# Block products of a seven-product matrix scheme chained in PSUM: banks copied by ScalarE and added to by further products, in place of sums on VectorE

## The chip, the cores and the metric

The kernel runs on one core of a Trainium2 chip. The metric is the device time of one execution in microseconds. A few words that are used throughout: PE is TensorE (the matrix unit), DVE is VectorE, ACT is ScalarE, POOL is GpSimd, SP is the engine that issues most transfers. PSUM is the memory that PE's products land in, in banks of 128 x 512 floats; SBUF is the working memory that everything else reads and writes.

## What is computed

The reference is one inference step of a two-layer decoder trunk on 512 prompt tokens and 64 sample tokens (576 in all), with a model width of 1024 and a branch width of 2048. Layer 0 is a gated short convolution, layer 1 an mLSTM block with a matrix memory. What matters here are the large projections:

```
# layer 0
b_gate, c_gate, xa, z = split(rmsnorm(x) @ w_in, 4)      # 1024 -> 4 x 2048
u = c_gate * xa;  y = b_gate * causal_conv(u) * silu(z);  x = x + y @ w_out
# layer 1
xm, z = split(rmsnorm(x) @ b_w_in, 2)
xc = silu(causal_conv(xm) + bias)
q = xc @ w_q;  k = xc @ w_k;  v = xm @ w_v               # 2048 -> 2048 each
... gates, chunkwise mLSTM with the states C, n, m, head norm, skip, silu(z), w_out ...
```

All arithmetic is in float32. PE multiplies rounded operands here, so each float32 operand is written as a rounded high part and a low part (`hi`, `lo`), and a product is three matmuls: hi by hi, hi by lo, lo by hi.

## The kernel before

Activations are kept transposed: a tile has 128 channels on the partitions and the 576 tokens along the free dimension. Everything is written for one core with a framework that gives each engine an instruction order of its own; the order is set by a list scheduler that works on the program's text and on its own estimates, so that an instruction of one engine can stand earlier or later than the source has it.

**Plain projections.** `products` (L222) runs 8 blocks of 128 input channels, three matmuls each, and each in two pieces (256 and 320 tokens), so 48 matmuls for one group of 1024 input channels and 128 output channels. The weights come by transfer as 128 x 1024 tiles (`wr`); ScalarE rounds them (`wh`, L202) and VectorE subtracts to get the low part (`wl`, L203). Four buffers hold `wh`, four `wl`, so a cast waits until PE has used the tile of four casts earlier.

**Pairs by seven block products.** For 38 pairs of output tiles the kernel uses a scheme that replaces eight half-size products by seven. Tokens are cut into two halves of 288 (`HT`), the input channels of a group of 1024 into even and odd blocks, and the two output tiles are the two rows of a 2 x 2 block matrix. `block_weights` loads the two weight tiles (a11, a12 in the first, a21, a22 in the second) and makes the sums s1 = a21 + a22 and s2 = s1 + a11 on VectorE (L286, L287); `mixed` and `forms` make the matching sums t1 to t4 of the activations. `block_pair` then runs the seven products of 12 matmuls each (4 blocks, three matmuls, 288 tokens; the inner function `product`, L304), every one with its own cast (`parts_of`, L250) and low part (L251). The results o11, o12 (first output tile) and o21, o22 (second) are, with P1 = a11 b11:

```
o11 = P1 + a12 b21
o12 = P1 - s2 t2 + s1 t1 + (s2 + a12) b22
o22 = s2 t2 + (a21 + a11) t3 - P1 - s1 t1
o21 = s2 t2 + (a21 + a11) t3 - P1 + a22 t4
```

(the signs are those of this kernel's sums). Before the change P1 is copied to SBUF (`p`, L311, ScalarE), products that only ever add are chained in one PSUM bank (`a12 b21` after P1 in `b0`, `t3` after `t2` in `b1`, `b22` after `t1` in `b2`), and everything else is added by VectorE from PSUM (L316 to L358).

There are three uses. In layer 0, 14 pairs (f = 1 to 14, `xs is None`): a pair gives c_gate and xa for 128 channels, then come two plain projections (`product(2)`, `product(3)`: z and b_gate) and the convolution, whose steps are taken from a list (`work`) by `run`, which `block_pair` calls between products. In layer 1, 8 pairs give v and 16 give k and q (the first of the 16 has `add`); there the other 1024 input channels are added by `plain` (L368), 48 matmuls per output tile into the same banks, and each finished tile is transposed on PE (`by_token`, L680 and L682) after GpSimd has spread the sample tokens (`spread`, L671).

PSUM is handed out by `accumulators`: a new pool per stage, with four banks of tag `blk` for the pairs. At the end of f = 0 in layer 0 and before the v stage a new pool with the same four banks is opened.

## Time and profile before

| | |
|---|---|
| three timed runs | 1714.5, 1715.65, 1722.03 us (median 1715.65) |
| the profiled execution's own time | 1715.56 us |
| its span, first to last instruction | 1713.5 us |
| PE busy in it | 1669.4 us (97%), 12315 matmuls |
| VectorE, ScalarE, GpSimd busy | 1105.3, 685.3, 107.7 us (65%, 40%, 6%) |
| mean granted PE clock | 0.987 of full speed |
| layer 0 pairs, from the profile's rows | about 51 to 375 us |
| v stage, then k and q stage | 612 to 820 us, 820 to 1284 us |

How to read it. Busy PE time says only that a matmul was in flight: matmuls overlap, one lasts about 294 ns while a new one starts every 133 ns or so (2260 of them in the 300 us from 100 to 400 us), and so the number of matmuls in a stretch of time tells more than the busy share. The trace writes a group of instructions as line, engine, operation, output from input, count, busy time, mean duration, idle time before it and what ended that idle time. A few matmul records can be missing from a trace.

### The profile page before, as it was taken

What the parts mean: (1) busy time and instruction counts of PE and PEld (TensorE: products, weight loads), DVE (VectorE), ACT (ScalarE), POOL (GpSimd) and SP (SyncE); (2) the same over time, 40 slices, a digit from 0 to 9 for tenths busy, and PEclk for the clock granted to TensorE, in tenths of its full rate; (3) what the DMA queues carried; (4) which work ended last, traced back from release to release, by engine and by line L of the source; (5) the groups of instructions that cost most, each with busy time, mean ns of one, the idle gap of its engine ahead of it and who ended that gap; (6) DMA issues with size and microseconds to landing.
All of it is one profiled execution on the core that took longest, in us unless ns stands there. A gap on an engine that the chain in (4) does not pass through costs nothing.

```text
span 1713.5 us, 30944 instructions
## 1 busy us (share of the span) xinstructions
PE 1669.4 (97%) x12315; PEld 1591.1 (93%) x12315; DVE 1105.3 (65%) x2078; ACT 685.3 (40%) x1252; POOL 107.7 (6%) x241
## 2 busy tenths in 40 slices
PE   9999999999999999999999999999999998898998
PEld 8999999999999999999999889899899787898898
DVE  6977877774436896555846345355468556778755
ACT  5433343342323553433534233233246455554421
POOL 0000000000000001000110010000021000000000
PEclk9999999999999999999999999999999899999999
DMA  5223322223432434434423552642745588797973
GB/s 193 74 83 99 103 86 85 90 73 137 141 115 87 141 122 151 138 111 154 152 88 120 188 178 87 219 154 62 271 161 195 201 280 286 247 361 249 362 276 105
DMA packets 107487, 275.23 MB, mean 161 GB/s; under 512 B 11056, under 2 KB 33456, under 8 KB 107344
## 3 DMA queue, kind: packets, MB, share of 16 engines
q1 hardware_dynamic: 91984, 255.95, 45.0%
q10 hardware_dynamic: 15360, 17.32, 2.9%
q8 instruction: 97, 1.59, 0.4%
q14 instruction: 46, 0.38, 0.1%
HBM read 211.13 MB, written 62.09 MB: 159 GB/s over the span
## 4 chain that ended last, share of the span: by engine, by line
PE 88%; DMA 5%; DVE 4%; ACT 2%; issue 1%; SPq 0%; POOL 0%; DVEq 0%; ACTq 0%; POOLq 0%
PE acc L222 34%; PE p L304 24%; PE p L368 16%; DMA c<-cs 2%; PE qa L759 2%; PE r L1122 2%; DMA cs_out<-c 1%; DMA wr<-wts 1%; PE g L661 1%; PE num L1175 1%; PE ta L680 1%; PE cp L1175 1%; PE num L1176 1%; PE s L778 1%; PE blk L368 1%
## 5 line engine op out<-in xcount | busy, mean ns | idle before, releaser
L222 PE MATMUL acc<-hi,wh 128*128 128x256 f32 (+1 forms) x1520 | 331.7, 299 | 11.1 <-ACT z L875 6.8
L222 PE MATMUL acc<-hi,wl 128*128 128x256 f32 (+1 forms) x1520 | 330.8, 299 | 0.0
L222 PE MATMUL acc<-lo,wh 128*128 128x256 f32 (+1 forms) x1520 | 330.2, 299 | 0.0
L202 ACT CAST wh<-wr 128x512 fp32r<-128x512 f32 x286 | 176.5, 621 | 328.6 <-PE acc L222 174.5
L304 PE MATMUL p<-hi,wh 128*128 128x288 f32 x968 | 286.7, 299 | 3.7 <-ACT wh L250 2.1
L304 PE MATMUL p<-lo,wh 128*128 128x288 f32 x968 | 284.5, 295 | 0.0
L304 PE MATMUL p<-hi,wl 128*128 128x288 f32 x968 | 279.2, 295 | 1.2 <-DVE wl L251 1.2
L222 PEld LDWEIGHTS acc<-hi,wh 128*128 128x128 f32 x1520 | 257.8, 191 | 16.0 <-ACT z L875 7.0
L203 DVE TENSOR_TENSOR wl<-wr,wh 128x512 fp32r<-128x512 f32 x286 | 195.8, 689 | 118.4 <-ACT wh L202 115.8
L222 PEld LDWEIGHTS acc<-hi,wl 128*128 128x128 f32 x1520 | 257.8, 191 | 2.2 <-issue 1.2
L222 PEld LDWEIGHTS acc<-lo,wh 128*128 128x128 f32 x1520 | 257.7, 191 | 0.7 <-issue 0.5
L250 ACT CAST wh<-wr 128x512 fp32r<-128x512 f32 x152 | 94.5, 622 | 258.4 <-PE p L368 116.7
L304 PEld LDWEIGHTS p<-hi,wh 128*128 128x128 f32 x968 | 181.9, 188 | 7.8 <-ACT wh L250 3.7
L304 PEld LDWEIGHTS p<-lo,wh 128*128 128x128 f32 x968 | 182.4, 188 | 0.0
L304 PEld LDWEIGHTS p<-hi,wl 128*128 128x128 f32 x968 | 179.9, 188 | 1.4 <-DVE wl L251 1.4
L368 PE MATMUL p<-hi,wh 128*128 128x288 f32 x736 | 169.9, 299 | 0.0
L368 PE MATMUL p<-lo,wh 128*128 128x288 f32 x736 | 166.9, 294 | 0.0
L368 PE MATMUL p<-hi,wl 128*128 128x288 f32 x736 | 166.4, 296 | 0.2 <-DVE wl L203 0.2
L251 DVE TENSOR_TENSOR wl<-ws,wh 128x512 fp32r<-128x512 f32 x114 | 78.7, 691 | 119.6 <-ACT wh L250 119.4
L250 ACT CAST wh<-ws 128x512 fp32r<-128x512 f32 x114 | 70.8, 621 | 187.8 <-PE p L368 108.3
L251 DVE TENSOR_TENSOR wl<-wr,wh 128x512 fp32r<-128x512 f32 x152 | 104.9, 691 | 52.3 <-ACT wh L250 50.5
L368 PEld LDWEIGHTS p<-hi,wh 128*128 128x128 f32 x736 | 120.8, 188 | 14.7 <-issue 11.2
(371 smaller groups left out, 2557.2 us busy)
## 6 DMA issues: line engine op xcount, KB each, us to landing
wr<-wts SPq DMA_DIRECT2D x222, 512.0 KB, 3.6
c<-cs SPq DMA_DIRECT2D x112, 512.0 KB, 5.8
cs_out<-c SPq DMA_DIRECT2D x64, 512.0 KB, 6.7
x<-xT SPq DMA_DIRECT2D x16, 288.0 KB, 4.1
xcs<-xc ACTq DMA_DIRECT2D x16, 288.0 KB, 2.2
x<-xcs SPq DMA_DIRECT2D x16, 288.0 KB, 4.1
x<-x1s SPq DMA_DIRECT2D x16, 288.0 KB, 4.5
ld<-xcs SPq DMA_DIRECT2D x16, 288.0 KB, 7.5
```

The costliest lines, as they stand in the source:

```text
L202: last_act[0] = nc.scalar.copy(hi, raw[:, 4 * i:4 * i + 4, :]).ins
L203: nc.vector.tensor_tensor(lo, raw[:, 4 * i:4 * i + 4, :], hi.bitcast(F32), ALU.subtract)
L222: nc.tensor.matmul(acc[:, o:o + j - i], a[:, k % 4, :], x[:, i:j], start=(first and k == 0 and p == 0), stop=(last and k == 7 and p == 2))
L250: last_act[0] = nc.scalar.copy(hi, src).ins
L251: nc.vector.tensor_tensor(lo, src, hi.bitcast(F32), ALU.subtract)
L304: nc.tensor.matmul(bank_, a[:, j, :], x, start=(start and j == 0 and i == 0), stop=(j == 3 and i == 2), skip_group_check=True)
L368: nc.tensor.matmul(b, a[:, k % 4, :], x[:, t:t + HT], start=bool(new) and k == 0 and i == 0, stop=(k == 7 and i == 2), skip_group_check=True)
L661: nc.tensor.matmul(g[32 * j:32 * j + 32, 0:b - a], w[:, 32 * j:32 * j + 32], tiles[j][:, a:b], start=True, stop=True)
L680: nc.tensor.transpose(pa[:, 128 * it:128 * it + 128], t[:, 128 * it:128 * it + 128], ident)
L759: nc.tensor.matmul(st["q"][32 * g:32 * g + 32, :], st["qp"][dt // 2][:, dt % 2, 128 * u + 32 * g:128 * u + 32 * g + 32], ct[g // 2][:, g % ...
L1122: nc.tensor.matmul(r, kst[2 * i + j][:, 128 * dt:128 * dt + 128], vst[:, 0:512], start=True, stop=True)
L1175: nc.tensor.matmul(acc[:, 256:512], w, b[:, 0:256], **ends)
```

## The change

In `block_pair` the order of the products is new and three banks hold running sums. P1 goes to bank `bx`. ScalarE writes its negative into a second bank (`by`, L310 of the new kernel), and the products with t2, t3 and t4 are added to `by` by PE one after the other; between them ScalarE copies what `by` holds at that time (`u` at L318, and `p` at L325 or a fourth bank `bv` at L328). s1 t1 goes to a third bank (`bw`), is copied to a new SBUF tile `m5` (L315), and gets the product with b22 added. Of the sums from PSUM two a pair remain on VectorE (six in the one pair with `add`). In the v, k and q stages both halves of `plain` now add to banks that are already in use (`bx` with `bw`, `by` with `bv`). `mark` writes one product into each of the four banks of a new pool, twice in the program, so that later products without a start flag add to what ScalarE wrote there.

```
-            b1 = block("p6")
-            product(b1, parts_of(s2), "t2", True)
-            b0 = block("p1")
-            product(b0, parts_of(a11), "b11", True)
-            nc.scalar.copy(p, b0)
+            bx = block("p1")
+            product(bx, parts_of(a11), "b11", True)
+            by = block("p6")
+            nc.scalar.activation(by, bx, AF.Copy, scale=-1.0)
             run(pops)
-            b2 = block("p5")
-            product(b2, parts_of(s1), "t1", True)
-            (sums of o12 from p and b1)
+            bw = block("p5")
+            product(bw, parts_of(s1), "t1", True)
+            m5 = X(HT, name="m5")
+            nc.scalar.copy(m5, bw)
+            run(pops)
+            product(by, parts_of(s2), "t2", False)
+            nc.scalar.copy(u, by)
+            tt(s2, s2, a12, ALU.add)
+            product(bx, parts_of(a12), "b21", False)
+            tt(a21, a21, a11, ALU.add)
+            run(pops)
+            product(by, parts_of(a21), "t3", False)
+            if xs is None or add:
+                nc.scalar.copy(p, by)
+            else:
+                bv = block("p7")
+                nc.scalar.copy(bv, by)
+            product(bw, parts_of(s2), "b22", False)
             run(pops)
-            product(b0, parts_of(a12), "b21", False)
...
-            b3 = block("p4")
-            product(b3, parts_of(a22), "t4", True)
-            tt(u, b1, p, ALU.subtract)
...
+            product(by, parts_of(a22), "t4", False)
...
+            if xs is None:
+                tt(o22, p, m5, ALU.subtract)
+                nc.scalar.copy(o11, bx)
+                tt(o12, bw, u, ALU.subtract)
+                nc.scalar.copy(o21, by)
+                return
+            plain(bx, bw, c1 + 1, xs, None)
+            nc.scalar.copy(o11, bx)
+            tt(o12, bw, u, ALU.subtract)
+            plain(by, bv, c2 + 1, xs, None)
+            nc.scalar.copy(o21, by)
+            tt(o22, bv, m5, ALU.subtract)
+
+        def mark(w, x):
+
+            for b in [block("mark") for _ in range(4)]:
+                nc.tensor.matmul(b, w, x, start=True, stop=True)
...
                 accumulators("acc0a", bufs=2)
+                mark(h1[0][0][:, 0:P], h1[0][0][:, 0:HT])
...
         accumulators("acc1", bufs=4)
+        mark(xm[0][0][:, 0:P], xm[0][0][:, 0:HT])
```

How the orders of the engines move is shown at three places. In the rows, a name's digits are buffer numbers, `p` is a PSUM bank of a pair, and the brackets name the engines that the instruction waits for. First PE at the end of f = 0 in layer 0, where the first pair begins. Before, `p_700` is the bank of s2 t2, `p_717` of P1 and `p_737` of s1 t1:

```order
L222 MATMUL acc_584<-hi_265,wl_592 128x320
L304 MATMUL p_700<-hi_405,wh_701 128x288 [waits PE_49,Activation_49]
L304 MATMUL p_700<-lo_406,wh_701 128x288
L304 MATMUL p_717<-hi_137,wh_718 128x288 [waits Activation_49]
L304 MATMUL p_717<-lo_138,wh_718 128x288
L304 MATMUL p_737<-hi_405,wh_738 128x288 [waits Activation_49]
```

After, on the same place, with `p_708` the bank of P1:

```order
L222 MATMUL acc_584<-hi_265,wl_592 128x320
L361 MATMUL mark_672<-hi_137 128x288 [waits Activation_49]
L361 MATMUL mark_673<-hi_137 128x288
L361 MATMUL mark_674<-hi_137 128x288
L361 MATMUL mark_675<-hi_137 128x288
L304 MATMUL p_708<-hi_137,wh_709 128x288 [waits PE_49]
L304 MATMUL p_708<-lo_138,wh_709 128x288
L304 MATMUL p_708<-hi_137,wl_710 128x288 [waits DVE_49]
```

The first pair used to begin with two matmuls each of three products, s2's first; now it begins with four marks and with the whole of P1, whose weights and activations need none of the sums.

Second, ScalarE in one pair in the middle of layer 0. Before, `pu` (L311) is the copy of P1, `cv` the convolution, `z` the gate, `wh` the weight casts:

```order
L250 CAST wh_2716<-wr_2496 128x512 [waits DMAHW3_49,PE_49,Activation_49]
L159 CAST hi_2622<-cv_2351 128x576 [waits DVE_49]
L250 CAST wh_2735<-wr_2496 128x512 [waits PE_49,Activation_49]
L311 COPY pu_2637<-p_2655 128x288 [waits PE_49]
L250 CAST wh_2755<-ws_2500 128x512 [waits PE_49,Activation_49]
L436 ACTIVATE cv_2630<-u_2629,cols 128x576 [waits DVE_49,Pool_49]
L202 CAST wh_2783<-wr_2631 128x512 [waits DMAHW5_49,PE_49,Activation_49]
L350 COPY cx_2635<-p_2655 128x288 [waits PE_49]
```

After, the same stretch of a pair (`p_2384` is the bank `by`, `p_2367` is `bx`, `p_2388` is `bw`; L310 writes `by`, L318 and L325 read it):

```order
L250 CAST wh_2446<-wr_2228 128x512 [waits DMAHW7_49,PE_49,Activation_49]
L310 ACTIVATE p_2384<-p_2367 128x288 [waits PE_49]
L159 CAST hi_2354<-cv_2083 128x576 [waits DVE_49]
L250 CAST wh_2463<-ws_2232 128x512 [waits PE_49,Activation_49]
L315 COPY m_2405<-p_2388 128x288 [waits PE_49]
L439 ACTIVATE cv_2359<-u_2358,cols 128x576 [waits DVE_49]
L250 CAST wh_2481<-wr_2228 128x512 [waits PE_49,Activation_49]
L318 COPY pu_2366<-p_2384 128x288 [waits PE_49]
L202 CAST wh_2512<-wr_2360 128x512 [waits DMAHW0_49,PE_49,Activation_49]
L202 CAST wh_2516<-wr_2360 128x512 [waits DVE_49,PE_49]
L202 CAST wh_2572<-wr_2362 128x512 [waits DMAHW1_49,PE_49]
L325 COPY pu_2366<-p_2384 128x288 [waits PE_49]
```

ScalarE's copies now stand between the casts and the two activations that wait for VectorE, and PE waits for three of them (L310, L318, L325) before it adds to `by`. PE's own order goes with that: the products run as P1, s1, s2, a12, s2 + a12, a21, that is with 12 matmuls between P1 and the first product on `by`, 24 between the first and the second, and the last (t4) stands some 27 matmuls behind the second, in the middle of the plain projection that follows.

Third, PE where one v pair ends and the next begins. Before, these transposes of the finished pair (`ta` from `v`, `tb` from the spread samples `dup`) come after three products of the next pair; `v_8244` and `v_8245` are its two output tiles:

```order
L304 MATMUL p_8596<-hi_6341,wl_8598 128x288
L680 MATMUL ta_8714<-cst,v_8244 128x128 [waits Activation_49]
L680 MATMUL ta_8714<-cst,v_8244 128x128 x3
L682 MATMUL tb_8715<-cst,dup_8552 128x128 [waits PE_49,Pool_49]
L682 MATMUL tb_8715<-cst,dup_8552 128x128 [waits Pool_49]
L680 MATMUL ta_8740<-cst,v_8245 128x128 [waits PE_49]
```

After, they come behind the first product (`p_8577` is the next pair's `bx`):

```order
L304 MATMUL p_8577<-hl_6357,wl_8579 128x288
L684 MATMUL ta_8730<-cst,v_8260 128x128 [waits Activation_49]
L684 MATMUL ta_8730<-cst,v_8260 128x128 x3
L686 MATMUL tb_8731<-cst,dup_8568 128x128 [waits Pool_49]
L684 MATMUL ta_8756<-cst,v_8261 128x128 [waits DVE_49,Activation_49]
L684 MATMUL ta_8756<-cst,v_8261 128x128
L684 MATMUL ta_8756<-cst,v_8261 128x128 [waits DVE_49]
```

The transposes moved 24 matmuls nearer to the end of the pair whose results they read, and the second tile, which is now the one finished last, is read only a few matmuls behind the first. Behind the last pair of the k and q stage the program's text is the same as before, and the orders differ there by groups of a few matmuls that stand earlier or later.

More of the change, by code (lines that the diff above doesn't have):

```diff
@@ L305, in product @@
                                          skip_group_check=True)
-            b1 = block("p6")
-            product(b1, parts_of(s2), "t2", True)
-            b0 = block("p1")
-            product(b0, parts_of(a11), "b11", True)
-            nc.scalar.copy(p, b0)
-            run(pops)
-            b2 = block("p5")
-            product(b2, parts_of(s1), "t1", True)
-            if add:
-                tt(o12, o12, b1, ALU.subtract)
-                tt(o12, o12, p, ALU.add)
-            else:
-                tt(o12, p, b1, ALU.subtract)
+            bx = block("p1")
+            product(bx, parts_of(a11), "b11", True)
+            by = block("p6")
+            nc.scalar.activation(by, bx, AF.Copy, scale=-1.0)
+            run(pops)
+            bw = block("p5")
[12 more added lines that the diff above has]
+                nc.scalar.copy(p, by)
+            else:
+                bv = block("p7")
+                nc.scalar.copy(bv, by)
+            product(bw, parts_of(s2), "b22", False)
             run(pops)
-            product(b0, parts_of(a12), "b21", False)
-            if add:
-                tt(o22, o22, b2, ALU.subtract)
-                tt(o22, o22, p, ALU.subtract)
-            else:
-                tt(o22, p, b2, ALU.add)
-            tt(a21, a21, a11, ALU.add)
-            tt(s2, s2, a12, ALU.add)
-            run(pops)
-            product(b1, parts_of(a21), "t3", False)
-            run(pops)
-            b3 = block("p4")
-            product(b3, parts_of(a22), "t4", True)
-            tt(u, b1, p, ALU.subtract)
-            if add:
-                tt(o22, o22, b1, ALU.add)
-            else:
-                tt(o22, b1, o22, ALU.subtract)
-            run(pops)
-            product(b2, parts_of(s2), "b22", False)
+            product(by, parts_of(a22), "t4", False)
+            run(pops)
             if mid:
@@ L345, in block_pair @@
             if add:
-                tt(o11, o11, b0, ALU.add)
-                tt(o21, o21, b3, ALU.add)
-                tt(o21, o21, u, ALU.add)
-            elif xs is None:
-                nc.scalar.copy(o11, b0)
-                tt(o21, b3, u, ALU.add)
-            else:
-                plain(b3, b1, c2 + 1, xs, False)
-                tt(o21, b3, u, ALU.add)
-                tt(o22, b1, o22, ALU.add)
-                plain(b0, b2, c1 + 1, xs, None)
-                nc.scalar.copy(o11, b0)
-            tt(o12, o12, b2, ALU.add)
+                tt(p, p, m5, ALU.subtract)
+                tt(o22, o22, p, ALU.add)
+                tt(o12, o12, u, ALU.subtract)
+                tt(o12, o12, bw, ALU.add)
+                tt(o11, o11, bx, ALU.add)
+                tt(o21, o21, by, ALU.add)
+                return
[4 more added lines that the diff above has]
+                nc.scalar.copy(o21, by)
+                return
+            plain(bx, bw, c1 + 1, xs, None)
[7 more added lines that the diff above has]
+                nc.tensor.matmul(b, w, x, start=True, stop=True)
         def plain(ba, bb, chunk, xs, start):
```

## The prediction, made before the changed kernel was run

> **What bounds the kernel now.** I read the page's head first, then a table by stretches of time, then the waits of PE, then the timeline at three places. The head says that PE is in flight for 97% of the span and the chain of work that ended last lies on it:
>
> ```profile
> PE 1669.4 (97%) x12315; PEld 1591.1 (93%) x12315; DVE 1105.3 (65%) x2078; ACT 685.3 (40%) x1252; POOL 107.7 (6%) x241
> PE 88%; DMA 5%; DVE 4%; ACT 2%; issue 1%; SPq 0%; POOL 0%; DVEq 0%; ACTq 0%; POOLq 0%
> ```
>
> Busy PE need not be fast PE, so I count matmuls per time. The first row covers the layer 0 pairs, the second a stretch of plain projections after them, the third v pairs (columns: us, PE, weight loads, DVE, ACT, POOL, clock):
>
> ```profile
> 100.00:400.00 300.00, 300.00 (x2260) 300.00 (x2260) 225.64 (x406) 117.45 (x199) 7.24 (x13) 1.00 0.30 92
> 425.00:450.00 25.00, 25.00 (x190) 25.00 (x189) 9.69 (x14) 7.28 (x12) 0.00 (x0) 1.00 0.38 122
> 687.00:712.00 25.00, 25.00 (x192) 25.00 (x191) 14.60 (x26) 9.81 (x17) 1.42 (x4) 1.00 0.46 140
> ```
>
> 300 us / 2260 = 132.7 ns a matmul with VectorE 75% busy, 25 / 190 = 131.6 ns with VectorE 39% busy. So PE issues at one rate, whatever VectorE does, and it is never short of work in the pairs. The waits of PE in the whole run (line, releaser, total us, times, longest) agree; these are the largest and all those near pairs over 1 us:
>
> ```profile
> PE acc L222 <- ACT z L875: 6.8, 1, 6.8
> PE num L1200 <- DVE vst L1025: 3.1, 1, 3.1
> PE r L1122 <- ACT y L1254: 2.7, 1, 2.7
> PE p L304 <- ACT wh L250: 2.1, 1, 2.1
> PE p L304 <- DVE wl L251: 1.2, 1, 1.2
> PE tb L682 <- POOL dup L671: 1.1, 1, 1.1
> ```
>
> The three long ones belong to the stage after the pairs, whose text is not touched. Near the pairs there are single waits, no wait that comes once a pair.
>
> **The change, part by part.** The sum is made against the profiled execution, 1715.56 us (span 1713.5 and 2.06 around it), which lies 0.09 under the median of 1715.65.
>
> *Matmuls.* Seven products of 12 a pair before and after; 8 marks are new. PE's work grows by 8 x 0.133 = 1.06 us.
>
> *Sums taken from VectorE, copies given to ScalarE.*
>
> ```profile
> L334 DVE TENSOR_TENSOR pu<-p,pu 128x288 f32<-128x288 f32 x38 | 17.3, 455 | 5.4 <-PE p L304 5.3
> L311 ACT COPY pu<-p 128x288 f32<-128x288 f32 x38 | 14.9, 392 | 0.0
> ```
>
> From the code: 6 sums to 2 in 14 pairs, 7 to 2 in 23, 10 to 6 in one, so 56 + 115 + 4 = 175 sums of 0.455 us, 80 us less on VectorE. ScalarE gets 151 more copies (226 for 75), 59 us at 0.392. Neither pays by itself: VectorE goes from 1105 to about 1025 us and ScalarE from 685 to 744, both far under the span, and PE waits for neither in the pairs. Gain taken: 0.
>
> *The chain through ScalarE in layer 0.* This is where the change could cost. PE must now wait for ScalarE three times a pair. In the trace of before, ScalarE in one pair (start, duration):
>
> ```profile
> 198.24 0.62 ACT L250 CAST wh<-wr 128x512 fp32r<-128x512 f32 x1 [1.10 <-PE p L304]
> 198.79 0.68 ACT L159 CAST hi<-cv 128x576 fp32r<-128x576 f32 x1
> 199.83 0.62 ACT L250 CAST wh<-wr 128x512 fp32r<-128x512 f32 x1 [0.36 <-PE p L304]
> 200.36 0.39 ACT L311 COPY pu<-p 128x288 f32<-128x288 f32 x1
> 201.41 0.62 ACT L250 CAST wh<-ws 128x512 fp32r<-128x512 f32 x1 [0.66 <-PE p L304]
> 201.94 0.77 ACT L436 ACTIVATE cv<-u,cols 128x576 f32<-128x576 f32 x1
> ```
>
> The casts released by PE start about 1.59 us apart (198.24, 199.83, 201.41), which is 12 x 0.133: each marks the end of a product. At 199.83 P1 has ended, a cast runs first, the copy of P1 ends at 200.75, 0.92 us after. In the new order a cast and the copy into `by` follow P1's end in the same way, and PE needs `by` 12 matmuls, 1.59 us, after it. Margin about 0.6 us. The copy now writes PSUM, which no row of before shows: the nearest rows are 0.392 (ScalarE, PSUM to SBUF) and 0.455 (VectorE on PSUM); I take 0.39, and up to 1.0 us it costs nothing. The Trainium skill says in "ScalarE: Activation LUTs", section "Step-by-step: what each stage is for", that ScalarE reaches PSUM sooner than SBUF; no run here shows it yet, and by it the copy would be no longer than 0.39 and the sum the same.
>
> The copy `u` has 24 matmuls, 3.18 us, from the end of the t2 product to the t3 product; ahead of it stand one cast and, earlier, the `cv` activation, which waits for VectorE's `u`: 0.77 + 0.62 + 0.39 = 1.78 us if all follow each other, margin 1.4. The copy `p` has 27 matmuls, 3.6 us, behind one cast: margin 2.5. What could eat these is a wait of ScalarE for VectorE, since its order is strict. Between 100 and 400 us that hardly happens:
>
> ```profile
> L436 ACT ACTIVATE cv<-u,cols 128x576 f32<-128x576 f32 x13 | 10.1, 774 | 1.6 <-DVE u L542 1.6
> L159 ACT CAST hi<-cv 128x576 fp32r<-128x576 f32 x13 | 8.8, 678 | 1.7 <-DVE cv L582 1.7
> ```
>
> 1.6 and 1.7 us over 13 of them, 0.13 us each, and VectorE will have 1.8 us less to do in a pair. Cost taken 0; if the cover is gone, 14 us for each us of overrun.
>
> *The ends of v, k and q pairs.* Transposes of the last tile now come 12 matmuls and some transposes, about 2.1 us, after its pair's end, in place of about 5.
>
> ```profile
> 716.47 0.62 ACT L250 CAST wh<-wr 128x512 fp32r<-128x512 f32 x1 [2.58 <-PE p L368]
> 716.74 0.45 DVE L358 TENSOR_TENSOR v<-v,p 128x288 f32<-128x288 f32 x1 [2.13 <-PE p L368]
> 717.00 0.40 ACT L357 COPY v<-p 128x288 f32<-128x288 f32 x1
> 717.32 1.34 POOL L671 COPY dup<-v 128x128 f32<-128x128 f32 x4 [23.86 <-ACT wh L250]
> ```
>
> The pair ended at about 716.4; copy and sum were done at 717.40, 1.0 us later, the spread of both tiles at 718.66, 2.3 us later, needed about 4.2 us after the end. Margins 1.1 and 2: cost 0. If ScalarE is late by another cast (0.62), still 0.
>
> *The first pair of layer 0.* Here something is to be had.
>
> ```profile
> 48.76 0.43 PE L222 MATMUL acc<-hi,wl 128*128 128x256 f32 x2
> 49.22 0.64 ACT L559 COPY cx<-acc 128x576 f32<-128x576 f32 x1 [1.91 <-PE acc L222]
> 51.26 0.40 PE L304 MATMUL p<-hi,wh 128*128 128x288 f32 x1 [2.07 <-ACT wh L250]
> 52.05 0.68 DVE L251 TENSOR_TENSOR wl<-ws,wh 128x512 fp32r<-128x512 f32 x1
> 55.05 0.42 PE L304 MATMUL p<-hi,wl 128*128 128x288 f32 x2
> 51.00:55.00 4.00, 3.74 (x15) 3.50 (x16) 4.00 (x8) 2.34 (x5) 0.00 (x0) 0.57 0.01 4
> 55.00:59.00 4.00, 4.00 (x32) 4.00 (x31) 3.87 (x9) 2.73 (x5) 0.59 (x1) 1.00 0.45 135
> ```
>
> After the last plain matmuls PE waits 2.07 us for a cast of s2, which VectorE must sum first, and then the granted clock is 0.57 for 4 us. From 49.05 (the next slot) to 55.05, 6.0 us, 15 matmuls are issued, worth 15 x 0.133 = 2.0: 4.0 us are lost. After, the marks wait for the copy that ends at 49.86 (0.85 lost), take 0.53, and P1 runs at once, since its weights need no sum. At 52.05 the s1 product needs its low part, which VectorE, with P1's low part put ahead, finishes at about 52.7 (52.05 + 0.68): about 0.4 lost. Together 1.8, gain 2.2 with the clock kept. Bounds: 0, if VectorE's chain is late for each product, and 3.1 (4.0 - 0.85), if the marks hide in it. If the clock still halves for about 3.4 us, 1.7 of the 2.2 go. The Trainium skill, "TensorE: Matmul & The Clock Gate", section "What's actually happening", has the clock drop after an idle window of some 3.4 us that runs freely, and rise after a busy one; the 0.57 behind the 2.07 us gap fits, and by it a gap of 0.85 keeps the clock, so the sum stays at 2.2.
>
> *The first v pair.* Its marks cost 0.5, and the first `by` product with t4 stands only 4 matmuls behind the first plain ones, so the copy `bv` (0.39 behind a cast) may hold PE 0.5. The single waits of 1.2 and 1.1 above may stay or go. Cost 1.0, from -1 to 2.
>
> Sum: -2.2 + 1.0 = -1.2, so 1714.4 us.
>
> **The rivals.**
>
> *ScalarE becomes a link of PE's chain (slower).* The place is layer 0, the price 14 us for each us by which the copy into `by` passes 1.0 us, or by which VectorE holds ScalarE longer than the margins above. With 1 us over in each pair: 1714.4 + 14 = 1728. For it: three waits a pair that weren't there, and ScalarE's strict order. Against: margins of 0.6, 1.4 and 2.5 us and the 0.13 us a time that ScalarE waits for VectorE.
>
> *The tail moves.* Behind the pairs the orders shift by a few matmuls, and that stage loses time to long waits and to a clock under 1:
>
> ```profile
> 1300.00:1400.00 100.00, 100.00 (x651) 85.18 (x650) 66.89 (x145) 49.40 (x106) 10.45 (x14) 0.93 0.61 205
> 1600.00:1714.00 114.00, 102.55 (x714) 97.06 (x713) 66.84 (x127) 30.17 (x59) 0.00 (x0) 0.94 0.65 235
> ```
>
> 100 x 0.07 and 114 x 0.06 are 7 us each of lost clock, beside waits of 6.8, 3.1 and 2.7. Losing two of the waits with some clock gains about 9 (1705), new ones cost as much (1723). For it: such losses hang on where gaps fall. Against: the work and nearly all of its order are the same.
>
> *VectorE's relief does show (faster).* If VectorE delayed PE in ways that the waits don't list, 80 us less might come back in part. Against: 132.7 and 131.6 ns at 75% and 39% load; 1.1 ns x 3192 pair matmuls is 3.5 us at most, 1711.
>
> **How the numbers follow.** Half a per cent, 8.6 us, is about what a measurement can tell here; the bounds are 1707.1 and 1724.2. My forecast and its near variants, the relief of 3.5 us among them, have 0.80. The tail in the good direction, or relief beyond that, 0.11. Slower: ScalarE's chain 0.06, the tail 0.03, together 0.09. The likeliest is 1714.4; the range reaches to the two tails, 1705 and 1723, and leaves out the stalled chain.
>
> **What would show it.** Right: about 2260 matmuls between 100 and 400 us again, no wait of PE for L310, L318, L325 or L328 that comes in every pair, VectorE near 1025 us and ScalarE near 744, the gap before the first pair under 1 us with the clock at 1.00 behind it. Wrong: fewer than 2200 matmuls there, a duration of L310 above 0.9 us, or a tail (from 1284 us to the end) that differs by more than 5 us.

## The result and the profile after

| | before | after |
|---|---|---|
| first timing, 9 runs each: median (lowest to highest) | 1717.58 (1714.5 to 1722.03) | 1726.92 (1723.15 to 1731.01) us |
| ratio after to before, 95% interval | | 1.0052 [1.0037, 1.0067] |
| second timing, on another occasion | 1718.09 | 1730.69 us; 1.0072 [1.0051, 1.0093] |
| profiled execution, its own time and span | 1715.56, 1713.5 | 1729.68, 1727.9 us |

The change makes the kernel 9 to 13 us slower, where 1714.4 was forecast and 1723 was the upper end. The head of the page of after:

```profile
PE 1679.3 (97%) x12323; PEld 1596.8 (92%) x12323; DVE 1045.3 (60%) x1903; ACT 727.0 (42%) x1403; POOL 100.6 (6%) x241
```

VectorE has 60 us less, ScalarE 42 us more, PE the 8 marks. The work moved as it was meant to. The layer 0 pairs run at their old rate (columns: us, PE, weight loads, DVE, ACT, POOL, clock, DMA share, GB/s):

```profile
100.00:200.00 100.00, 100.00 (x755) 100.00 (x754) 72.15 (x124) 45.99 (x88) 2.92 (x5) 1.00 0.30 94
200.00:300.00 100.00, 100.00 (x755) 100.00 (x754) 72.15 (x124) 44.50 (x86) 2.33 (x4) 1.00 0.30 95
```

There are 755 matmuls in each 100 us, where before had 755 and 756, and a pair still takes 23.91 us. The new copies from bank to bank (L310 and L328) last as long as the copy of P1 to SBUF did in before (392 ns), and as long as the new one to SBUF (L315):

```profile
L315 ACT COPY m<-p 128x288 f32<-128x288 f32 x38 | 15.0, 394 | 3.7 <-PE p L304 3.7
L310 ACT ACTIVATE p<-p 128x288 f32<-128x288 f32 x38 | 14.9, 392 | 0.4 <-PE p L304 0.4
L328 ACT COPY p<-p 128x288 f32<-128x288 f32 x23 | 9.0, 392 | 1.1 <-PE p L304 1.1
```

The waits of PE, of which the second and the last shown here are new (the dots stand for others):

```profile
PE acc L222 <- ACT z L880: 7.1, 1, 7.1
PE blk L371 <- ACT v L352: 6.8, 1, 6.8
PE num L1205 <- DVE vst L1030: 3.1, 1, 3.1
...
PE p L304 <- ACT p L328: 1.4, 1, 1.4
```

To see where time goes, I compare when the same pair matmul starts in each trace (all pair matmuls counted in PE's order). Differences to before, us:

| start of a matmul | before | after | difference |
|---|---|---|---|
| first of the second pair of layer 0 | 77.0 | 74.2 | -2.8 |
| in the 13th of the 14 pairs of layer 0 | 346.4 | 343.5 | -2.8 |
| in the last v pair | 804.8 | 801.0 | -3.7 |
| in the second k and q pair | 856.9 | 861.8 | +4.8 |
| last plain matmul of k and q | 1284.0 | 1298.9 | +14.9 |

Each trace is one execution, and stretches that the change leaves alone differ between executions too. In the experiments below that keep before's layer 0, the second pair starts from 1.5 us earlier to 0.9 us later than here. Before's own second v pair took 28.4 us, with a wait of 1.1 us for `dup` that no other trace lists, where the six other kernels with the old form of that pair take 26.9. So a difference to this one trace is good to some 3 us, and what a stage costs is read better from its own length.

The first pair's gap is the 0.73 us ahead of the marks, and the clock stays up behind it:

```profile
49.63 0.80 PE L361 MATMUL mark<-hi 128*128 128x288 f32 x4 [0.73 <-ACT cx L562]
50.26 0.29 PE L304 MATMUL p<-hi,wh 128*128 128x288 f32 x1
```

```profile
52.00:56.00 4.00, 4.00 (x33) 4.00 (x32) 4.00 (x7) 2.41 (x6) 0.33 (x1) 1.00 0.01 2
```

From the last plain matmul ahead of the first pair to the second pair, before takes 28.1 us and after 25.6, like the ten other traces with the new pairs and a single copy in layer 0. Of the three experiments that keep before's layer 0, with the same wait of 2.1 us, one takes 28.7 us and two take 27.1, and in these two the clock did not fall behind the wait (the k and q pairs alone, and before with groups cut):

```profile
51.00:55.00 4.00, 4.00 (x26) 3.36 (x26) 4.00 (x7) 2.44 (x5) 0.00 (x0) 1.00 0.03 6
51.00:55.00 4.00, 3.39 (x20) 2.74 (x21) 4.00 (x8) 3.05 (x6) 0.00 (x0) 1.00 0.02 4
```

So the gain is 1.6 us where before keeps its clock, and 2.5 to 3.1 where it does not.

By the table, then, about 3 us are gained at the start (0.3 of them ahead of that matmul) and two losses follow: **A**, some 8 to 9 us at the step from the v pairs to the k and q pairs, and **B**, 10 us spread through the k and q pairs. Behind them the stage of the tail takes 429.5 us in before and 428.9 in after.

**A.** ScalarE of after around that step (start, duration, what ended the idle time):

```profile
817.51 0.43 ACT L273 CAST hl<-x 128x288 fp32r<-128x288 f32 x1
817.85 0.67 ACT L159 CAST hi<-x 128x576 fp32r<-128x576 f32 x1
820.32 0.67 ACT L159 CAST hi<-fa 128x576 fp32r<-128x576 f32 x1 [1.81 <-DVE fa L258]
821.06 0.67 ACT L159 CAST hi<-fb 128x576 fp32r<-128x576 f32 x1
821.64 0.43 ACT L273 CAST hl<-x 128x288 fp32r<-128x288 f32 x1
821.97 0.67 ACT L159 CAST hi<-x 128x576 fp32r<-128x576 f32 x1
822.54 1.07 ACT L688 ACTIVATE ta<-ta 128x512 f32<-128x512 f32 x2
...
823.51 0.40 ACT L352 COPY v<-p 128x288 f32<-128x288 f32 x1
...
823.78 0.42 ACT L355 COPY v<-p 128x288 f32<-128x288 f32 x1
```

and PE on both sides of its wait:

```profile
816.73 0.42 PE L371 MATMUL p<-hi,wl 128*128 128x288 f32 x2
823.96 0.61 PE L371 MATMUL blk<-hi,wh 128*128 128x288 f32 x1 [6.80 <-ACT v L352]
```

The last v pair also calls `mid`, here `mixed_blocks`, which prepares the sums of activations for the k and q pairs, with 16 casts on ScalarE, some of which wait for VectorE's `fa` and `fb`. `o11`'s bank was complete 48 matmuls ahead of 816.9, at about 810.5 (48 x 0.133 = 6.4 us), but ScalarE's copy of it (L352) stands behind all the casts in ScalarE's list. The first plain product of the next pair needs that bank. VectorE's own two reads of this pair stand later still, behind its sums for `mid`:

```profile
825.47 0.45 DVE L353 TENSOR_TENSOR v<-p,pu 128x288 f32<-128x288 f32 x1
825.83 0.45 DVE L356 TENSOR_TENSOR v<-p,m 128x288 f32<-128x288 f32 x1
```

So it is the place in the list, behind the work of `mid`, that holds the banks, on either engine; PE met ScalarE's first. Why the scheduler put the reads there, and not ahead as in before, no run shows. Before, VectorE freed two banks early and only the third stood among the casts:

```profile
816.41 0.45 DVE L354 TENSOR_TENSOR v<-p,pu 128x288 f32<-128x288 f32 x1
816.78 0.45 DVE L355 TENSOR_TENSOR v<-p,v 128x288 f32<-128x288 f32 x1
```

```profile
821.28 0.68 ACT L159 CAST hi<-fa 128x576 fp32r<-128x576 f32 x1 [2.94 <-DVE fa L258]
821.86 0.62 ACT L202 CAST wh<-wr 128x512 fp32r<-128x512 f32 x1
822.38 0.39 ACT L357 COPY v<-p 128x288 f32<-128x288 f32 x1
```

The lower clock behind the wait costs more (windows of after):

```profile
816.00:820.00 4.00, 1.16 (x9) 0.92 (x7) 3.92 (x8) 2.39 (x5) 0.00 (x0) 0.93 0.44 155
820.00:824.00 4.00, 0.04 (x1) 0.04 (x1) 4.00 (x8) 3.61 (x8) 0.00 (x0) 0.50 0.29 98
824.00:828.00 4.00, 4.00 (x17) 3.98 (x18) 2.85 (x7) 0.20 (x1) 1.44 (x4) 0.50 0.69 197
828.00:832.00 4.00, 4.00 (x28) 4.00 (x28) 0.45 (x2) 1.07 (x2) 0.00 (x0) 0.79 0.00 0
```

17 and 28 matmuls in 4 us, where full speed gives 30: 15 x 0.133 = 2.0 us more, so 6.8 + 2.0 is about 9, of which a little comes back in the next pair.

**B.** No wait explains the k and q pairs: from the second of them on, PE's listed waits are 1.1 us in before and 0.5 in after, all for c tiles. One head with its windows, in before and in after (matched at the ends of the same pairs):

```profile
921.40:1042.50 121.10, 120.59 (x908) 109.69 (x908) 58.50 (x106) 37.67 (x68) 11.08 (x31) 1.00 0.48 160
```

```profile
927.10:1051.00 123.90, 123.85 (x908) 110.50 (x907) 51.97 (x87) 42.06 (x84) 10.72 (x31) 1.00 0.48 157
```

The same 908 matmuls at full clock, 2.8 us longer. What differs is PE's order. `query_state` issues four matmuls 32 columns wide, which run beside each other in the array (the trace has two records for each). In before's list all 24 such groups of the three heads are whole; in after's, 6 are cut into three and one by a matmul of a pair. A whole group and the two parts of a cut one in PE's rows of after, each with the row behind it (a group's four matmuls are x8, three are x6, one is x2):

```profile
994.40 1.06 PE L764 MATMUL qa<-c,qp 128*32 128x512 f32 x8
995.40 0.40 PE L371 MATMUL p<-hi,wh 128*128 128x288 f32 x1
...
1007.33 1.06 PE L764 MATMUL qa<-c,qp 128*32 128x512 f32 x6
1008.32 0.40 PE L304 MATMUL p<-hi,wh 128*128 128x288 f32 x1
...
1010.62 1.04 PE L764 MATMUL qa<-c,qp 128*32 128x512 f32 x2
1011.60 0.54 PE L371 MATMUL p<-hi,wl 128*128 128x288 f32 x2
```

Four take 1.00 us, three 0.99, one 0.98: a matmul that is cut off its group costs as much as the whole group, about 1.07 us with 0.09 more ahead of it (0.22 instead of 0.13 from the matmul before). The Trainium skill says in "TensorEngine Tiling (Array Packing)", section "Key Properties", that different tiles can run their matmuls in parallel; the trace agrees, and shows that this holds only for neighbours in the list. The gates' groups (L661 in before) are cut too, 9 runs into 12. By these prices the 6 cuts of narrow groups cost 6.4 us; the rows of the gates' groups add about 0.7 us a head, 2 us; the three heads lose 9.3 in all. Why the new order of the pairs leads the scheduler to cut the groups is not shown.

### The profile page after: what moved, and what is told of

It reads as the page before. It is cut to its first block, busy times and chain, and to the rows that moved or that the text cites. A ratio compares the mean times of both kernels' runs of the same rounds, so it can differ in the third digit from the quotient of the medians.

```text
span 1727.9 us, 30952 instructions
## 1 busy us (share of the span) xinstructions
PE 1679.3 (97%) x12323; PEld 1596.8 (92%) x12323; DVE 1045.3 (60%) x1903; ACT 727.0 (42%) x1403; POOL 100.6 (6%) x241
## 4 chain that ended last, share of the span: by engine, by line
PE 88%; DMA 5%; DVE 4%; ACT 2%; issue 1%; SPq 0%; DVEq 0%; ACTq 0%
PE acc L222 32%; PE p L304 24%; PE p L371 17%; PE qa L764 2%; DMA wr<-wts 2%; DMA cs_out<-c 2%; PE cp L1180 1%; PE cp L1181 1%; PE r L1127 1%; DMA c<-cs 1%; PE g L665 1%; DVE c L1128 1%; PE blk L371 1%; PE ta L684 1%; PE s L783 1%
## 5 line engine op out<-in xcount | busy, mean ns | idle before, releaser
L304 PE MATMUL p<-hi,wh 128*128 128x288 f32 x968 | 288.2, 298 | 1.4 <-ACT p L328 1.4
L304 PE MATMUL p<-lo,wh 128*128 128x288 f32 x968 | 284.7, 294 | 0.0
L371 PE MATMUL p<-hi,wh 128*128 128x288 f32 x736 | 159.8, 298 | 0.1
L371 PE MATMUL p<-lo,wh 128*128 128x288 f32 x736 | 159.8, 295 | 0.0
```

The costliest lines, as they stand in the source:

```text
L304: nc.tensor.matmul(bank_, a[:, j, :], x, start=(start and j == 0 and i == 0), stop=(j == 3 and i == 2), skip_group_check=True)
L371: nc.tensor.matmul(b, a[:, k % 4, :], x[:, t:t + HT], start=bool(new) and k == 0 and i == 0, stop=(k == 7 and i == 2), skip_group_check=True)
```

## The experiments

Theory: A and B, as above, and a gain of 3 us at the first pair. Rival: ScalarE's copies between banks cost a little in every pair. "Last plain" is the start of the last plain matmul of k and q against before's 1284.0; it leaves out the tail, whose time differs by 10 us between the profiled runs; the spread of some 3 us between executions is in it. Each ratio is to before timed on the same occasion. Where the expectations speak of 15 pairs, layer 0 has 14 and the k and q stage 16.

**One stage at a time.** The old block pair was kept beside the new one and chosen by stage, with the mark of the stage:

```
-            block_pair(c1, c2, ...)
+            (block_pair if c1 < 128 else block_pair_old)(c1, c2, ...)    # v alone; the other two alike
```

New pairs in layer 0 alone:

> The new block pair in the 15 pairs of layer 0 alone, with its mark ahead of them; the v, k and q pairs as before. The theory puts the loss in two places of the later pairs and leaves the first pair's gain: the v pairs begin 3 to 4 us earlier than before, and the end comes 3 us earlier (1714.5 us against 1717.6, ratio 0.998). The rival, that ScalarE's copies between banks hold TensorE a little in every pair, gives 0.3 to 0.5 us for each of the 15 pairs, 5 to 7 us, less the first pair's 3: 2 to 4 us slower than before (ratio 1.001 to 1.002), and a cadence in layer 0 longer than 23.91 us.

Measured: 1710.17 against 1718.97, 0.9955 [0.9939, 0.9971]. The second pair starts 3.2 us early, the cadence is 23.91 us, and in the last v pair it is 4.7 us ahead. The rival falls for layer 0. The timed gain is larger than the trace's 3 to 5 us; see the end.

New pairs in v alone:

> The new block pair in the 8 v pairs alone, with its mark ahead of them. The theory: one wait of TensorE of 6 to 7 us at the step from the last v pair to the first k and q pair, behind ScalarE's casts for the next stage, and some 2.5 us at half clock behind it; first v pair 0.7 us; in all 9 to 10 us slower than before (ratio 1.0055 in the profiled runs; 1.004 to 1.006 in the timed ones), and the other v pairs as long as before. The rival, a small cost in every pair, gives 0.5 us for each of 8 pairs, 4 us, spread evenly, and no such wait.

Measured: 1726.21, 1.0048 [1.0030, 1.0066]; last plain +6.0. The wait is there to the tenth:

```profile
PE blk L441 <- ACT v L352: 6.8, 1, 6.8
```

New pairs in k and q alone:

> The new block pair in the 15 k and q pairs alone. The theory: TensorE's list in the three heads with work between the matmuls has the groups of four narrow matmuls for the sample queries cut into three and one twice a head, and the gates' groups of eight into two and six; each cut costs 0.8 to 1.1 us, 2.8 us a head and 8 to 9 us in all (ratio 1.005), with no wait of TensorE and nothing in the fourth head. The rival, ScalarE's copies at the ends of pairs, spreads 8 us over all 15 pairs, 0.55 us each, also in pairs whose groups are whole, and shows TensorE waiting for the copies.

Measured: 1726.76, 1.0045 [1.0032, 1.0059]; last plain +9.0. At the start of that stage, up to which its text is that of before, it was -3.0, which is the spread between executions; from the second k and q pair on 10.6 us are lost. The list has the same cuts as after, 6 and 3, and no wait of PE for a copy of these pairs.

**The copies ahead of the casts.** In the last v pair `mid()` was moved behind the copies and sums:

```
-            if mid:
+            if mid and c1 >= 128:
                 mid()
...
             tt(o22, bv, m5, ALU.subtract)
+            if mid and c1 < 128:
+                mid()
```

> The changed kernel with the last v pair's preparation of the next stage (the forms of the xc tiles) written behind the pair's last copies and sums, so that ScalarE's copy that frees the bank stands ahead of the casts. The theory: the wait of 6.8 us and the half clock behind it go, 9 to 10 us faster than the changed kernel, 3 to 5 us slower than before by the profiled runs (the k and q pairs' part stays). Rival: the casts wait for tiles loaded from DRAM and the next pair needs their results, so TensorE stands at the first product of the next pair instead: the same 7 to 9 us at another row, no gain.

Measured: 1737.37, 1.0109 [1.0090, 1.0127], slower than after itself (1.0052 and 1.0072); last plain +18.3. The theory's forecast failed. The wait for L352 is gone, another has come:

```profile
PE g L667 <- ACT ta L690: 9.3, 1, 9.3
```

`ta` is the copy of the transposed v tile out of PSUM; now it runs at 840.09, behind the last of the casts (839.52), and the gates need a bank. The rival had the outcome, no gain and a wait of this size at another row, but named the next pair's first product and the casts' results: PE waits for a bank, and the casts hold whatever reader of a bank is behind them.

**Undoing A, and holding the groups.** Four kernels: the changed kernel with the groups of `query_state` held together; with the last v pair in its old form; with both and the gates held too; and before with 21 of its 24 groups cut (the edits are shown in part).

```
+                with tc.issue_after(plain_mm[0]):          # each narrow matmul behind the last plain one
+                    narrow_end[0] = nc.tensor.matmul(st["q"][32 * g:32 * g + 32, :], ...
...
+                        with tc.issue_after(narrow_end[0]) if narrow_end[0] else nullcontext():
                             ... next step of plain
...
+            (block_pair_old if mid and c1 < 128 else block_pair)(c1, c2, ...)     # last v pair as before
...
+                fourth.append(lambda: narrow(1))       # before, groups cut: the fourth a step later
```

> The changed kernel with the four narrow matmuls of each group for the sample queries held together in TensorE's list, and the plain product's next step behind them: 24 runs of four in the three heads again, as before, where the changed kernel has 18 runs of four, 6 of three and 6 of one; the gates' groups stay cut. The theory, by the trace's rows of these groups: 6 cuts less, 2.2 us a head, 6 to 7 us in all; 1720 us where the changed kernel has 1727 (ratio to before 1.001 to 1.002). The rival, that the k and q pairs lose to ScalarE's copies, gives no gain (1.005).

Measured: 1730.54, 1.0069 [1.0051, 1.0086]; last plain +15.3. No gain, although the list has 24 whole groups. Held in their places the groups wait for their tiles:

```profile
PE qa L769 <- DMA c<-cs: 5.8, 7, 1.6
```

In after's list matmuls of the pairs stand there instead, which are ready, and the same freedom cuts the groups. The rival's number came out, but not its reason: PE waits for tiles, and for no copy of these pairs.

> The changed kernel with the last v pair alone in its form of before (five products in banks opened for it, seven reads by VectorE, two banks free early). The theory: the wait of 6.8 us at the first k and q pair and the half clock behind it go, 9 to 10 us faster than the changed kernel, 1717 to 1718 us (ratio to before 1.000). The rival, that the wait only moves to another reader of a bank on ScalarE behind the casts, as in the run with the forms last, gives 1727 us again, with a wait of 7 to 9 us at another row.

Measured: 1724.99, 1.0034 [1.0021, 1.0047]; last plain +5.2, 9.8 us earlier than after. The step runs at full speed:

```profile
816.00:820.00 4.00, 4.00 (x33) 4.00 (x32) 3.96 (x9) 3.41 (x7) 2.52 (x4) 1.00 0.22 87
820.00:824.00 4.00, 4.00 (x33) 4.00 (x32) 1.82 (x5) 0.12 (x1) 0.15 (x1) 1.00 0.69 270
```

but the timed medians, from two occasions, differ by 2 us only, which the last four runs take up.

> The changed kernel with the last v pair as before, the groups for the sample queries held together, and the gates' groups too (held behind the plain product's step). The theory: both losses go, 9.5 and 6.6 us and 1 to 2 for the gates, and the first pair's gain stays: 1709 to 1711 us, as the run with the new pairs in layer 0 alone (ratio to before 0.995). The rival, small costs of ScalarE's copies in the v, k and q pairs: 1714 to 1718.

Measured: 1722.91, 1.0031 [1.0015, 1.0047]; last plain +8.6, with waits for c tiles of 6.0 us in 7, and one of 2.3 us for VectorE's `tb` at the step to the k and q pairs. Missed mainly for the reason of the first of these.

> The kernel before with the fourth narrow matmul of 21 of the 24 groups set one step later, so that each of these groups is a run of three and a run of one; the same matmuls, nothing else changed. The theory: 0.8 to 1.1 us a cut, 17 to 23 us slower than before (ratio 1.010 to 1.0135). If a cut cost only the matmul's own turn between its neighbours (0.13 us, as one of 288 columns), 3 us (1.002).

Measured: 1743.10, 1.0137 [1.0120, 1.0155]: 24.2 us for 21 cuts, 1.15 us each; by the last plain matmul 21.1 us, 1.0 each, and from the second k and q pair on 23.2 us, 1.1 each. No wait for c tiles is listed. The price of a cut is so shown in a kernel without any of the change; the edit also holds the groups to a place in the list, which here brought no wait.

**The first pair, ScalarE's margin, the c tiles.** Two parts of the gain alone, the copy L310 made four times, and c tiles asked for one group ahead:

```
+                mark(h1[0][0][:, 0:P], h1[0][0][:, 0:HT])        # before, marks only
...
+            if xs is None: P1 ahead of the t2 product             # before, order only (abridged)
...
+            for _ in range(4):                                    # new pairs in layer 0 alone
                 nc.scalar.activation(by, bx, AF.Copy, scale=-1.0)
...
+                    work.append(lambda ...: (ahead(i=i + 1), query_state(heads[h], units_[i], i)))
+                    work.append(lambda: None)
```

> The kernel before with the four marks ahead of the first pair of layer 0 and nothing else. If the marks' place in the list brings the first pair's gain (they fill the wait, so the clock stays up), the second pair begins 2 to 3 us earlier than the 77.0 us of before. If the gain comes from the order of the products, the wait only follows the marks and the second pair begins 0 to 1 us earlier. For the time: the run with the new pairs in layer 0 alone was 8.8 us faster by its timed medians where its trace is 3.2 us ahead at the second pair and until the k and q pairs; if the first pair's gap alone were behind all of it, a kernel without the gap would be 8 us faster; if the rest is spread of the end of the kernel, 1 to 3 us.

Measured: 1715.59, 0.9981 [0.9966, 0.9996]; second pair 0.8 us early, which is within the spread between executions. From the last plain matmul to the second pair it takes 27.1 us, as the two kernels with before's layer 0 whose clock did not fall.

> The kernel before with the first two products of the layer 0 pairs exchanged (the product with the plain block a11, which waits for a cast only, ahead of the one with the sum s2), five banks and VectorE's sums as before, no marks. The theory that the first pair's gain is one of order: the second pair begins 2 to 3 us earlier than 77.0, the later pairs keep 23.91 us, 2 to 3 us faster in the trace, 0.998; if the first gap is behind all of the 8.8 us of the run with layer 0 alone, 0.995. The rival, that the chained banks and fewer sums of VectorE make the gain: no change.

Measured: 1716.77, 0.9992 [0.9982, 1.0002]; second pair 0.9 us early, 26.9 us from the last plain matmul. Neither alone gives the 25.6 of the new pairs: with marks alone PE waits 0.7 and 0.6 us, with P1 first 0.7 and 1.1; in after only 0.7. What is left may come from the chained order, in which s1 (one sum) is wanted second and s2 (two sums) third; marks and P1 first together, without that order, were not run.

> The new pairs in layer 0 alone, with the negated copy of the first product's bank into the second product's bank made four times over in all the new pairs (so 15 of layer 0), 1.18 us more of ScalarE on the chain. The margin in the trace is some 0.6 us (the copy ends at 148.51, the product that adds to its bank starts at 149.07): by it 0.6 us of each of the 15 pairs' copies shows, a cadence of 24.5 us instead of 23.91, 8 to 9 us slower than with the single copy (ratio to before 1.000). The rival, that ScalarE's list has slack enough that TensorE takes other work meanwhile: no change (0.9955).

Measured: 1739.68, 1.0121 [1.0101, 1.0142]. By the start of the v stage the trace is 24 us behind the one with the single copy, 1.7 us a pair. The side of the margin was right, the size not:

```profile
PE p L304 <- ACT m L316: 18.0, 13, 1.7
```

The wait, 1.4 us in 13 pairs, is booked to the copy m5, which came among the four. ScalarE in one pair:

```profile
206.22 0.39 ACT L311 ACTIVATE p<-p 128x288 f32<-128x288 f32 x1
206.55 0.65 ACT L159 CAST hi<-cv 128x576 fp32r<-128x576 f32 x1
207.10 0.39 ACT L311 ACTIVATE p<-p 128x288 f32<-128x288 f32 x1
207.43 0.60 ACT L250 CAST wh<-ws 128x512 fp32r<-128x512 f32 x1
207.94 0.39 ACT L311 ACTIVATE p<-p 128x288 f32<-128x288 f32 x1
208.26 0.39 ACT L316 COPY m<-p 128x288 f32<-128x288 f32 x1
208.55 0.39 ACT L311 ACTIVATE p<-p 128x288 f32<-128x288 f32 x1
```

The scheduler set other work between the copies, so the last one ends 2.7 us after the first began, where four in a row would take 1.6.

> The changed kernel with the last v pair as before, the groups for the sample queries held together, and their c tiles asked for one group earlier, with one step free between two groups, so that a group need not wait for its tiles. The theory: the cuts' 6.6 us go without the waits for c tiles of 5.8 us that came in their place when the groups were held without loads ahead: at the last k and q product 5 to 7 us earlier than with only the last v pair as before, that is 2 us earlier to 1 us later than before (ratio 0.999 to 1.000). The rival, that the tiles' rate (2 MB for two groups) and not the order sets the pace: waits for c tiles again, 1.003.

Measured: 1718.55, 1.0001 [0.9986, 1.0015]; last plain +0.9, 4.2 us earlier than with only the last v pair as before, a little less than expected, since the clock fell once in its first v pair. From the second k and q pair on it takes 437.3 us, 7.4 less than that kernel and within what the old k and q pairs take. No wait for c tiles is listed. So the cuts' cost can be won back, if the tiles come early enough.

**A and B in and out, timed together.** Open was whether the losses are the same in every execution. All four kernels below have the new pairs in layer 0 and in seven v pairs; the last v pair is new (A) or old, the k and q pairs are new (B) or old.

> The changed kernel once more, beside the next three on the same chip: layer 0 new, and of the two losses both (the last v pair new: A; the k and q pairs new: B). The theory that both losses are set by the lists of instructions and so the same in every execution: TensorE's wait at the first k and q pair again 6.8 us, the last plain product of the k and q pairs again 14 to 16 us later than before's 1284.0, and the time 1725 to 1728. The rival, that the wait depends on transfers and varies from one execution to the next, gives another length for it here, by 2 us or more.

> New pairs in layer 0 and in seven of the eight v pairs; the last v pair and the k and q pairs as before: neither A nor B. The theory: the last plain product 3 to 4 us earlier than before's, the groups whole, no wait at the step to the k and q pairs; 1712 to 1715 us (ratio 0.997, as the new pairs of layer 0 alone give, less 0.7 us at the first v pair). The rival, that the seven v pairs cost by themselves: 1717 and more.

> New pairs in layer 0 and in all v pairs, the k and q pairs as before: A alone. The theory: the wait of 6.8 us at the first k and q pair, the last plain product 5 to 7 us later than before's, and 9 to 10 us slower than the run with seven v pairs. If the end of the kernel takes up part of what comes late, less: 4 to 7 us in the timed medians.

> The changed kernel with the last v pair as before, once more: B alone. The theory: the last plain product 5 to 6 us later than before's, 9 to 10 us faster than the changed kernel of this call and 8 to 9 us slower than the run with seven v pairs. If the end of the kernel takes up part of it: 2 us faster than the changed kernel, as in the first such run.

Measured, with 1718.09 for before:

| | timed median | ratio | last plain |
|---|---|---|---|
| neither | 1711.89 | 0.9962 [0.9950, 0.9975] | -1.5 |
| A | 1720.78 | 1.0032 [1.0018, 1.0046] | +5.8 |
| B | 1723.16 | 1.0031 [1.0019, 1.0044] | +6.9 |
| A and B (after) | 1730.69 | 1.0072 [1.0051, 1.0093] | +16.6 |

```profile
PE blk L371 <- ACT v L352: 6.8, 1, 6.8
```

The wait is 6.8 us in after's second profile as in the first, in A alone, and in the other two traces that have it. A costs 8.9 us without B and 7.5 with it; B costs 11.3 without A and 9.9 with it. The end of the kernel does not take them up, and the 2 us of the earlier comparison, from runs on different occasions, were too small. The last plain matmul of the same kernel differs by 1.7 us between its two profiles (14.9 and 16.6; 5.2 and 6.9); waits for c tiles, 0.6 to 2.8 us in all in these four, are of that size.

The lengths of the two stretches in all traces say the same. From the start of the last v pair to the second k and q pair, the five traces with the new last pair and the wait take 60.9 to 62.1 us, and eleven with the old one 52.8 to 54.3. (The run with the forms last takes 64.8, the one with both mends 57.0.) From there to the last plain matmul, the six with new k and q pairs and free groups take 444.7 to 447.3 us, the eight with the old ones and whole groups 434.9 to 439.3. So A is about 8 us and B about 10.

## Why the prediction was wrong

- *The base, 1715.56 us:* it is one execution, and the three runs at hand had a median of 1715.65. In the larger sets before's median is 1717.6 to 1719.0, so 2 to 3 us of the distance between forecast and measurement is not of the change.
- *Matmuls, 1.06 us:* 8 more records, as said. But "seven products of 12 a pair before and after" priced k and q by count alone. One step that failed is there, since a matmul's price was taken not to depend on its neighbours in PE's list: in the three heads of k and q the list has 9 more runs of narrow and gates' matmuls, which cost B, about 10 us. The price of a cut stood in no row that I had looked at; the comparison of the orders showed the cuts.
- *VectorE and ScalarE, gain 0:* right, as no place shows PE gaining by it. Busy time is 1045 and 727 us where 1025 and 744 were given, since it counts the overlap of instructions once (the cast at 817.51 lasts 0.43, the next starts at 817.85); the durations added up fall by 83 us on VectorE and rise by 58 on ScalarE, where 80 and 59 were forecast.
- *The chain through ScalarE in layer 0, cost 0:* right. Cadence and the 0.392 us of the copy came as said; a PSUM target was not quicker than SBUF (0.394). The kernel with the copy four times shows that the cover is thin: 1.7 us a pair are lost once it is gone.
- *The ends of v, k and q pairs, cost 0:* this is the other step that failed, by A, 8 to 9 us. The margins of 1.1 and 2 us were read at one ordinary v pair (716 us) and held for 23. The last v pair is not ordinary: its `mid` puts 16 casts into ScalarE's list, and with the new form the reads of all four banks come behind the work of `mid`, where before VectorE had freed two banks at 816 to 817 us. The prediction named transposes as those who wait for the copies, and not the next pair's first product, which waits for the bank.
- *The first pair of layer 0, gain 2.2:* right in kind: 2.5 us against before's trace, with a gap of 0.7 us and the clock at 1.00 behind it. The size was in part luck. The 4.0 us that it takes as lost include the fall of the clock, and in two other executions the same wait of 2.1 us was followed by no fall; against those the gain is 1.6. That the 0.57 behind the gap "fits" was read too surely: the cost of this gap is not the same each time. (Its 0.85 lost ahead of the marks is 0.81 by its rows, which hardly moves the sum.)
- *The first v pair, cost 1.0:* the marks cost 0.7 us ahead of it, and the pair itself takes 26.0 us instead of 24.5, with the wait for L328 of 1.4. The second v pair gives this back: 25.2 us, where other executions of the old form take 26.9. So 0.7 is left.
- *The rivals:* the slower one named ScalarE's lateness, at the wrong place: layer 0, a little in each pair, instead of one long wait at a step between stages. The tail is within 1 us.
- *The signs:* 2251 matmuls from 100 to 400 us, no wait in every pair, a gap under 1 us with the clock at 1.00, the tail unchanged: nearly all that was named as a sign of being right came (VectorE and ScalarE at 1045 and 727 us), and none that was named as a sign of being wrong, beside a loss of 9 to 13 us. The signs looked at layer 0 and at the tail, and none at the step between v and k or at PE's list in the k and q pairs.

The best version is the one with neither loss: new pairs in layer 0 alone (0.9955 [0.9939, 0.9971]) or in layer 0 and seven v pairs (0.9962 [0.9950, 0.9975]). Both beat before and after. That gain, 6 to 9 us in the timed medians, is larger than the 3 to 5 us that the traces show ahead of the tail. The profiled execution of before was among its shorter ones (1715.56, median 1718). Part of the gain lies in the clock: the median granted clock of the timed runs is 0.989 for both kernels, and 0.9865 and 0.986 for the runs of before beside them, which is 4 to 5 us of 1710 by estimate (0.0025 and 0.003 of it). One fall as in before's first pair, 0.57 for 4 us, would make 1.7 of these (4 x 0.43); where the rest comes from is not settled.

## What to carry to other kernels

A change of which engine reads a PSUM bank, or when, gives the read a new place in an engine's list: look, at each step between stages, at what stands ahead of it there, not only at one ordinary round. And where a change reorders the matmuls, count the runs of narrow ones that share the array: a group that is cut costs a second full pass, with no wait in the profile to show it. And when a gain of a few us is read from one trace of before, look first at how much the stretches that nothing touched differ between traces.

## What the runs showed of the hardware

- A PE wait of 6.8 us is followed by 0.50 of the clock until about 829.7, nearly 6 us after work resumed. Shorter waits cost clock in some executions only. The 2.1 us ahead of the first pair were followed by 0.57 for 4 us in before and by 0.82 and 0.75 in the run with the v pairs alone, but by 1.00 in two other kernels; a wait of 1.4 to 1.5 us in the first v pair left 1.00 in after and brought 0.85 and 0.72 for 4 us each in the run with the loads ahead. Waits of 0.7 us, and of about 1.4 us once in every pair (the copy four times), left it at 1.00. The Trainium skill, "TensorE: Matmul & The Clock Gate", section "What's actually happening", has the clock fall after at least one idle window of about 3.4 us; the 6.8 us agree, while the 2.07 us of before are shorter than that and still cost clock there.
- A ScalarE copy from one PSUM bank to another of 128 x 288 takes 0.392 us, the same as from PSUM to SBUF (0.394).
- Four matmuls of 32 columns by 512 that follow each other in PE's list take 1.00 us to the next matmul, three 0.99, one alone 0.98.
- From the last plain matmul of k and q to the end, with the same 2744 matmul records in each trace, the profiled runs took from 426.7 to 436.7 us.
